# Delta rule: a longer pipeline for the keys' chain, and one merge for both halves of a head

## The chip, the cores and the metric

The kernel runs on one core of one Trainium2 chip. The time is device microseconds of one execution; it is given as the median of several runs. TensorE (PE) multiplies, VectorE (DVE), ScalarE (ACT) and GpSimd (POOL) do the elementwise work, and SyncE (SP) issues all DMAs from one queue, in order. Each engine works through its own queue in order and waits there for the others.

## The reference

Four residual layers on x of 1024 x 1024 in float32: a gated convolution, forgetting attention, gated DeltaNet, sliding-window attention. The change is in the third layer alone. For each of 8 heads of width 128, in 16 chunks of 64 tokens:

```python
qkv = silu(causal_conv(h @ w_in[:, :3072], w_conv))        # q, k, v; q and k are then normalized
L = where(strict, (k_beta @ k.T) * decay, 0)               # per chunk, 64 x 64
T = triangular_solve(eye + L, eye)                         # the inverse
u, w = T @ v_beta, T @ (k_beta * exp(g_cum))
# scan over the chunks
v_new = u_c - w_c @ state
o = qd @ state + qk_c @ v_new
state = state * exp(g_last) + kd.T @ v_new
...
return (rms_norm(o) * w_onorm * silu(z)) @ w_out
```

## The kernel before

**Units.** A projection of 128 features for half of the tokens (512) is eight *units*. A unit is three matmuls of 128 x 512 (L159 to L161): float32 numbers are split into a high and a low part, and high x high, high x low and low x high are added in PSUM. The order of TensorE is written by hand: generators yield after each unit, and `layer_gdn` takes from them in turn. In the steps of phase one the orders of ScalarE and GpSimd are the program's too. VectorE's and SP's orders are a scheduler's, fixed before the run.

**Phase one** makes the keys. Step n (1 to 15; 16 and 17 drain) treats one half of one head, `keys(hd, h)`. Its stages: eight units, then on ACT a copy (L1297) and a product (L1305) and on VectorE three convolution products (L1307); ACT's tanh and VectorE's last product (L1314); then four transposes on TensorE (L1322), which wait for L1314. ACT sums squares (L1330), VectorE (L1361), GpSimd (L1362, a power) and VectorE again (L1364) make the factors; a small transpose (L1379) turns the factors into a row that goes through DRAM and comes back broadcast; GpSimd multiplies it by the decay (L1387); TensorE forms k k^T (L1392), VectorE multiplies (L1394), and the result L goes to DRAM. The stages of several halves are in flight, each a step or two behind the next. Between them stand units of the gate z (`zfill`, weights in the tiles `cv` and `QK`), whose next weights are loaded and split on the way (ACT casts the high part, GpSimd subtracts, L1676).

**The solve.** The 32 x 32 diagonal blocks of eight halves (four heads) lie over 128 partitions. VectorE inverts them row by row: a product of two SBUF tensors (L1428), a reduction (L1431), 80 of them for a block of heads in 71 yields, then a copy (L1434). `advance(b, n)` takes n yields. The first block of heads is solved in steps 10 to 15; the result goes to DRAM (L1433, L1435) and is read back by `loads` (L1459, L1461). Clearing the tile for the second block (L1417) waits until the first result has been written out.

**Phase two** runs the scan, head by head, one half at a time. `prepare` is the fill between the scan's steps: units of q and v, and `merge`, which makes 128 x 128 inverses out of the 32 x 32 blocks in four groups of small matmuls (L1477; L1482 and L1485; L1493; L1498) with VectorE or ACT between them. The scan's hops (L1591, L1596, L1604, then L1623 and L1624) hang together through VectorE; a quota of fill, `FILL // HOPS` = 100 with 64 for a unit, stands between two hops. Each half has its own merge.

Of the kernel before, what the change touches and what calls it, by code (L numbers as in the profile page):

```python
# [16 lines left out]
ALU = mybir.AluOpType  # L17
# [1169 lines left out]
class Gdn:  # L1187
# [249 lines left out]

    def advance(self, b, n):

        if b not in self.sol:  # L1440
            self.sol[b] = self.solve(b, self.U)
        for _ in range(n):
            if next(self.sol[b], 0) == 0:
                break

    def loads(self, hd, h):

        k, p, nc = self.k, self.p, self.nc
        LT = p.tile([P, HT], F32, name="LT", bufs=3)
        nc.sync.dma_start(out=LT.rearrange("p (c i) -> p c i", i=P), in_=self.chunks(self.LT_d[hd][h]))  # L1450
        TT = p.tile([P, 4, P], F32, name="TT", bufs=NB)
        nc.gpsimd.memset(TT, 0.0)
        T1 = p.tile([P, 4, 64], F32, name="T1", bufs=1)
        nc.gpsimd.memset(T1, 0.0)
        base = (hd % 4) * 32 + h * 16
        for q in range(4):
            qs = slice(32 * q, 32 * q + 32)
            src = [self.T_d[hd // 4][t][base:base + 16, :].rearrange("(c q) (r n) -> q r c n", q=4, n=32)[q] for t in range(2)]
            nc.sync.dma_start(out=TT[qs, :, qs], in_=src[1])  # L1459
            if q < 3:  # L1460
                nc.sync.dma_start(out=T1[qs, :, 32:64] if q == 1 else T1[qs, :, 0:32], in_=src[0])  # L1461
        kT = p.tile([P, HT], F32, name="kT", bufs=NB)
        nc.sync.dma_start(out=kT, in_=self.kT_d[hd][h])
        return LT, TT, T1, kT

    def merge(self, LT, TT, T1):

        k, p, nc = self.k, self.p, self.nc
        LT = LT.rearrange("p (c i) -> p c i", i=P)
        ps = k.psum("pj")  # L1470
        v32 = lambda a, rows: ps[rows, a:a + 128].rearrange("p (c n) -> p c n", n=32)
        fst = [slice(64 * q, 64 * q + 32) for q in range(2)]
        snd = [slice(64 * q + 32, 64 * q + 64) for q in range(2)]
        Q = p.tile([P, 4, 32], F32, name="Q", bufs=1)
        for q in range(2):
            for c in range(4):
                nc.tensor.matmul(v32(0, snd[q])[:, c, :], LT[fst[q], c, snd[q]], T1[fst[q], c, 0:32], start=True, stop=True)  # L1477
        for q in range(2):
            nc.vector.tensor_scalar(Q[snd[q]], v32(0, snd[q]), -1.0, None, op0=ALU.mult)
        yield 16  # L1480
        for c in range(4):
            nc.tensor.matmul(v32(128, snd[0])[:, c, :], TT[snd[0], c, snd[0]], Q[snd[0], c, :], start=True, stop=True)  # L1482
        for q in range(2):
            for c in range(4):
                nc.tensor.matmul(v32(128, fst[q])[:, c, :], Q[snd[q], c, :], TT[snd[q], c, snd[q]], start=True, stop=True)  # L1485
        nc.scalar.copy(T1[snd[0], :, 0:32], v32(128, snd[0]))
        for q in range(2):
            nc.scalar.copy(TT[fst[q], :, snd[q]], v32(128, fst[q]))
        yield 40
        lo, up = slice(0, 64), slice(64, 128)  # L1490
        v64 = lambda rows: ps[rows, 256:512].rearrange("p (c n) -> p c n", n=64)
        for c in range(4):
            nc.tensor.matmul(v64(up)[:, c, :], LT[lo, c, up], T1[lo, c, :], start=True, stop=True)  # L1493
        Q6 = p.tile([P, 4, 64], F32, name="Q6", bufs=1)
        nc.vector.tensor_scalar(Q6[up], v64(up), -1.0, None, op0=ALU.mult)
        yield 18
        for c in range(4):
            nc.tensor.matmul(v64(lo)[:, c, :], Q6[up, c, :], TT[up, c, up], start=True, stop=True)  # L1498
        nc.scalar.copy(TT[lo, :, up], v64(lo))
        yield 44  # L1500


    def wload(self, j, hd):
# [3 lines left out]
    def prepare(self, hd, h):  # L1507

        k, p, nc = self.k, self.p, self.nc
        hs = slice(h * HT, (h + 1) * HT)  # L1510
        LT, TT, T1, kT = self.ahead.pop(0)
        E = p.tile([P, HT], F32, name="LT", bufs=3)
        nc.sync.dma_start(out=E, in_=self.E_d[hd][h])
        eg = p.tile([P, HT], F32, name="LT", bufs=3)
        nc.sync.dma_start(out=eg, in_=self.eg_d[hd:hd + 1, hs].broadcast_to([P, HT]))
        mg = self.merge(LT, TT, T1)

        def mixed(steps, vals, every):
# [12 lines left out]

        first = hd == 0
# [6 lines left out]
        yield from mg  # L1539
        if h:  # L1540
            self.wload(2, hd + 1)
        nxt = hd * 2 + h + 1
        if nxt < 16:
            self.ahead.append(self.loads(nxt // 2, nxt % 2))
# [12 lines left out]
        self.vals.append((v, hd, h))  # L1557
        self.prep[hd, h] = [kT, TT, q, sq, QK]
# [89 lines left out]

FILL = 1300
HOPS = 13  # L1650
ZF = 5
LAG = 5

MORE = (25, 0, -25)
# [2 lines left out]
def layer_gdn(k, out):  # L1657
    with k.tc.tile_pool(name="gd", bufs=1) as p:
# [52 lines left out]
        with k.tc.manual_schedule(engines={E_.PE}):  # L1711
# [13 lines left out]
            stage(0, 5)  # L1725
            take(gts)
            stage(0, 4)
            take(zfill, ZF + 5)
            take(gts)
            take(zfill, 3)  # L1730
            take(gts)
# [3 lines left out]

            def step(n):
                hd, h = n // 2, n % 2
                dec = decs.pop(0)
# [9 lines left out]
                if n > 1:  # L1748
                    take(dec)
                if 10 <= n < 16:  # L1750
                    g.advance(0, 6)
                take(cur, 5)
                stage(n - 1, 2)
                take(cur, 4 if n < 16 else 3)
                if n == 1:
                    take(late, 2)
                    take(dec)
                stage(n - 1)
                stage(n - 2)
                if n < 14 and not h:  # L1760
                    kraw.append([k.raw_wk(g.w_in[j * 512:(j + 1) * 512, 1024 + (hd + 1) * P:1024 + (hd + 2) * P], P) for j in range(2)])
                if 10 <= n < 16:
                    g.advance(0, 3)
# [4 lines left out]
                decs.append(g.decay((n + 1) // 2, (n + 1) % 2) if n < 15 else none)  # L1768
                take(decs[0])
                stage(n - 2)  # L1770
                stage(n - 1)
                if 10 <= n < 16:
                    g.advance(0, 3)
# [5 lines left out]
            decs = [g.decay(0, 1)]  # L1779
            take(decs[0])  # L1780
            kraw = [[k.raw_wk(g.w_in[j * 512:(j + 1) * 512, 1024 + P:1024 + 2 * P], P) for j in range(2)]]
            with k.tc.manual_schedule(engines={E_.Activation, E_.Pool}):
                for n in range(1, 16):
                    step(n)
            g.ahead.append(g.loads(0, 0))
            for j in range(2):
                g.kd_load(j)
            step(16)
            step(17)
            stage(15)  # L1790
# [95 lines left out]
```

## Time and profile before

| | us |
|---|---|
| median of 3 runs | 2152.6 (2151.2 to 2155.11) |
| profiled execution, its own time | 2149.09 |
| its span in the trace | 2147.4 |
| TensorE busy | 2078.8 (97% of the span) |
| VectorE busy | 1323.6 (62%) |
| ScalarE busy | 992.1 (46%) |
| GpSimd busy | 836.8 (39%) |
| the chain that ended last | TensorE 74%, VectorE 13%, ACT 4%, DMA 4%, issue 3% |

The phase one of the third layer lies at about 1077 to 1268 us of the span, phase two at about 1268 to 1600. Matmuls are pipelined: the end of a row is modelled, so the time that one takes is read from the start of one row to the start of the next.

### The profile page before, as it was taken

Reading aid. Unit: us, or ns where it says so; the run is one execution under the profiler, and the core shown is the slowest. Engines: PE = TensorE matmul, PEld = TensorE weight load, DVE = VectorE, ACT = ScalarE, POOL = GpSimd, SP = SyncE. Lnnn points to the kernel's source line nnn. Section 1 sums busy time; section 2 is a strip of 40 time slices with the busy share of each in tenths; the row PEclk is TensorE's granted clock in tenths of the full one; section 3 lists DMA queues with packets and bytes.
Section 4 is the critical chain, followed back from the end, with each engine's and each line's share of the span. In section 5 each row is a group of like instructions: output and inputs, shape, how many; then the busy total and the mean of one; then the engine's idle time right before and its main releaser. Section 6 shows DMA issues by size and latency. Waiting matters only on the chain.

```text
span 2147.4 us, 33391 instructions
## 1 busy us (share of the span) xinstructions
PE 2078.8 (97%) x11717; PEld 1748.3 (81%) x11717; DVE 1323.6 (62%) x2748; ACT 992.1 (46%) x2483; POOL 836.8 (39%) x721
## 2 busy tenths in 40 slices
PE   7999999999999999999999789999999999999998
PEld 5887888788898989888688677878888888878888
DVE  7657655544535355475455967775565568888874
ACT  6333334433433233454366443434443446666764
POOL 2244544731221221236356552322324545445630
PEclk9999999999999999999999999999999999999999
DMA  7122213741222321236256553342325521121134
GB/s 237 50 69 84 64 59 119 224 95 41 47 38 44 40 51 31 58 95 187 75 159 195 157 171 96 87 122 78 102 80 164 168 66 49 46 54 50 45 89 148
DMA packets 288366, 205.70 MB, mean 96 GB/s; under 512 B 41381, under 2 KB 245574, under 8 KB 288198
## 3 DMA queue, kind: packets, MB, share of 16 engines
q1 hardware_dynamic: 288198, 203.56, 33.9%
q8 instruction: 93, 1.52, 0.3%
q14 instruction: 75, 0.61, 0.1%
HBM read 154.87 MB, written 43.38 MB: 92 GB/s over the span
## 4 chain that ended last, share of the span: by engine, by line
PE 74%; DVE 13%; ACT 4%; DMA 4%; issue 3%; POOL 1%; SPq 0%; ACTq 0%; POOLq 0%; DVEq 0%
PE ps_pj L159 15%; PE ps_pj L160 15%; PE ps_pj L161 15%; PE ps_sc L248 2%; PE ps_sc L250 2%; PE ps_sc L249 2%; PE ps_pj L248 1%; PE ps_pj L249 1%; PE ps_pj L250 1%; PE ps_tr L835 1%; DVE sp L1428 1%; DVE cu L1307 1%; DVE lg L1153 1%; PE ps_pj L743 1%; PE ps_pj L745 1%
## 5 line engine op out<-in xcount | busy, mean ns | idle before, releaser
L159 PE MATMUL ps_pj<-hhi,whi 128*128 128x512 f32 (+1 forms) x1712 | 698.8, 409 | 3.5 <-ACT hhi L411 1.4
L160 PE MATMUL ps_pj<-hlo,whi 128*128 128x512 f32 (+1 forms) x1712 | 669.2, 391 | 7.2 <-DVE hlo L416 3.9
L161 PE MATMUL ps_pj<-hhi,wlo 128*128 128x512 f32 (+1 forms) x1712 | 669.0, 391 | 0.0
L143 POOL TENSOR_TENSOR wlo<-wraw,whi 128x512 fp32r<-128x512 f32 x296 | 404.4, 1373 | 615.9 <-ACT whi L142 584.9
L161 PEld LDWEIGHTS ps_pj<-hhi,wlo 128*128 128x128 f32 x1712 | 321.8, 188 | 68.9
L160 PEld LDWEIGHTS ps_pj<-hlo,whi 128*128 128x128 f32 x1712 | 323.3, 189 | 61.6 <-DVE hlo L416 5.1
L159 PEld LDWEIGHTS ps_pj<-hhi,whi 128*128 128x128 f32 x1712 | 323.1, 189 | 59.7 <-issue 2.5
L142 ACT CAST whi<-wraw 128x512 fp32r<-128x512 f32 x304 | 185.9, 617 | 312.1 <-PE ps_pj L160 172.7
L1307 DVE SCALAR_TENSOR_TENSOR cu<-cb,taps,cu 128x512 f32<-128x512 f32 x144 | 135.7, 942 | 12.3 <-ACT cu L1305 10.5
L1159 POOL TENSOR_TENSOR lg<-lg,st 128x512 f32<-128x512 f32 (+1 forms) x64 | 63.7, 996 | 122.7 <-DVE st L1158 117.3
L888 ACT ACTIVATE lg<-lg,mx 128x512 f32<-128x512 f32 (+2 forms) x96 | 58.7, 613 | 64.0 <-DVE mx L883 63.6
L1156 ACT ACTIVATE lg<-lg,st 128x257 f32<-128x257 f32 (+1 forms) x128 | 63.1, 494 | 49.2 <-DVE st L1153 49.0
L840 ACT CAST phi<-ps_tr 128x512 fp32r<-128x512 f32 (+1 forms) x80 | 40.6, 544 | 94.3 <-PE ps_tr L835 94.2
L461 DVE TENSOR_TENSOR y<-ps_pj,xr 128x512 f32<-128x512 f32 x56 | 38.5, 687 | 64.0 <-PE ps_pj L161 57.5
L841 DVE TENSOR_TENSOR plo<-ps_tr,phi 128x512 fp32r<-128x512 f32 (+1 forms) x80 | 49.5, 633 | 42.5 <-ACT phi L840 42.5
L469 DVE TENSOR_TENSOR acc<-acc,hf 128x512 f32<-128x512 f32 x49 | 48.5, 990 | 41.2 <-ACT hf L468 41.2
L143 POOL TENSOR_TENSOR wlo<-wr,whi 128x512 fp32r<-128x512 f32 x36 | 48.0, 1333 | 59.0 <-ACT whi L142 54.7
L1428 DVE TENSOR_TENSOR sp<-sT,sU 128x504 f32<-128x504 f32 (+18 forms) x80 | 57.0, 713 | 6.3 <-DMA sU<-gLT 5.1
L1153 DVE CUSTOM_DVE_ANT_0 lg<-ps_sc,band,sk 128x256 f32<-128x256 f32 (+1 forms) x128 | 55.0, 464 | 5.0 <-PE ps_sc L1148 3.4
L291 DVE SCALAR_TENSOR_TENSOR y<-y,ps_pj 128x512 f32<-128x512 f32 x48 | 32.7, 681 | 38.6 <-ACT y L290 38.6
L743 PE MATMUL ps_pj<-whi,hhi 128*128 128x256 f32 x192 | 54.8, 285 | 0.0
L744 PE MATMUL ps_pj<-wlo,hhi 128*128 128x256 f32 x192 | 54.6, 285 | 0.0
(448 smaller groups left out, 4613.5 us busy)
## 6 DMA issues: line engine op xcount, KB each, us to landing
xd<-y SPq DMA_DIRECT2D x64, 256.0 KB, 3.4
wraw<-in_fox_w_in_dram SPq DMA_DIRECT2D x60, 256.0 KB, 4.2
xr<-xd SPq DMA_DIRECT2D x56, 256.0 KB, 2.8
wraw<-in_gdn_w_in_dram SPq DMA_DIRECT2D x52, 256.0 KB, 3.7
wraw<-in_conv_w_in_dram SPq DMA_DIRECT2D x40, 256.0 KB, 3.0
wraw<-in_swa_w_in_dram SPq DMA_DIRECT2D x40, 256.0 KB, 2.9
wraw<-in_conv_w_out_dram SPq DMA_DIRECT2D x32, 256.0 KB, 4.9
wraw<-in_fox_w_out_dram SPq DMA_DIRECT2D x32, 256.0 KB, 2.8
```

The costliest lines, as they stand in the source:

```text
L142: nc.scalar.copy(hi[:, :, :cols], raw[:, :, :cols])
L143: (eng or nc.gpsimd).tensor_tensor(lo[:, :, :cols], raw[:, :, :cols], hi[:, :, :cols].bitcast(F32), op=ALU.subtract)
L159: nc.tensor.matmul(o, hi, xhi, start=(c == 0), stop=False)
L160: nc.tensor.matmul(o, hi, xlo, start=False, stop=False)
L161: nc.tensor.matmul(o, lo, xhi, start=False, stop=(c == NC_ - 1))
L248: nc.tensor.matmul(ps, whi[:, c, :], xhi, start=start and c == 0, stop=False, skip_group_check=True)
L249: nc.tensor.matmul(ps, whi[:, c, :], xlo, start=False, stop=False, skip_group_check=True)
L250: nc.tensor.matmul(ps, wlo[:, c, :], xhi, start=False, stop=stop and c == 3, skip_group_check=True)
L743: nc.tensor.matmul(ps, xhi, whi, start=(c == 0), stop=False)
L1153: nc.vector.tensor_tensor_reduce(lg[:, u, :n], ps[:, u, :n], band[:, 2 * P - n:], 1.0, sk[:, hd:hd + 1], ALU.add, ALU.min, st[:, 0, u:u + 1])
L1307: eng.scalar_tensor_tensor(u, cb[:, j:j + HT], tap(j), u, op0=ALU.mult, op1=ALU.add)
L1428: nc.vector.tensor_tensor(v, T[:, n0:i, n0:n1].rearrange("p j n -> p n j"), U[:, n0:i, i].unsqueeze(1).broadcast_to([P, n, m]), op=ALU.mult)
```

## The change

In phase one the keys' chain gets longer. The transposes of the half before now come after all eight units of the step's own half, and k k^T is formed in the third step behind the half's own, where it was in the second. The gate units between are no longer five in each step: `ZF` = 3 up to step 9, and `ZL` = 8 from step 10 on, in two groups of four. The solve's yields are spread by the table `ROWS` over three places of a step, 65 in steps 10 to 15, the rest in step 16. The decay's rows are loaded in the step itself, not one ahead.

In phase two both halves of a head are merged in one pass through the four groups, while the first half's v is projected. So the second half's blocks are loaded in the middle of the first half's q, the tile T1 has two buffers, and the tiles Q and Q6 go (T1 takes their place). E and eg are loaded at other places.

```diff
     def advance(self, b, n):
-        if b not in self.sol:
+        if n and b not in self.sol:
...
-        T1 = p.tile([P, 4, 64], F32, name="T1", bufs=1)
+        T1 = p.tile([P, 4, 64], F32, name="T1", bufs=2)
...
-    def merge(self, LT, TT, T1):
+    def merge(self, sets):
...
+        sets = [(LT.rearrange("p (c i) -> p c i", i=P), TT, T1, k.psum("pj")) for LT, TT, T1 in sets]
+        for LT, TT, T1, ps in sets:
+            for q in range(2):
+                for c in range(4):
+                    nc.tensor.matmul(v32(ps, 0, snd[q])[:, c, :], LT[fst[q], c, snd[q]], T1[fst[q], c, 0:32], ...)
+            for q in range(2):
+                nc.vector.tensor_scalar(T1[snd[q], :, 0:32], v32(ps, 0, snd[q]), -1.0, None, op0=ALU.mult)
+        yield 16 * len(sets)
...
+        yield 40 * len(sets)
...
+        yield 18 * len(sets)
...
+        yield 44 * len(sets)
...
     def prepare(self, hd, h):
-        mg = self.merge(LT, TT, T1)
...
+                if n == load:
+                    self.ahead.append(self.loads(hd, 1))
...
-        q = yield from mixed(self.conv_steps(self.w[0], hd, h, "qT", 2), LAG, 0 if first else 2)
+        q = yield from mixed(self.conv_steps(self.w[0], hd, h, "qT", 2), LAG, 0, 0 if h else LAG + 1)
         if h:
             self.wload(0, hd + 1)
-        if not first:
-            yield from mg
-        v = yield from mixed(self.conv_steps(self.w[2], 16 + hd, h, "cv", 2), 0, 2)
+        else:
+            mg = self.merge([t[:3] for t in self.ahead])
+        v = yield from mixed(self.conv_steps(self.w[2], 16 + hd, h, "cv", 2), 0, 0 if h else 2)
         yield from mg
...
-ZF = 5
+ZF, ZL = 3, 8
+ROWS = {10: (0, 6, 6), 11: (4, 4, 4), 12: (4, 4, 4), 13: (4, 3, 3), 14: (4, 3, 3), 15: (3, 3, 3), 16: (99,)}
...
             def step(n):
-                stage(n - 2)
-                stage(n - 3)
...
-                take(cur, 5)
-                stage(n - 1, 2)
-                take(cur, 4 if n < 16 else 3)
...
+                take(cur, 2)
+                stage(n - 3)
+                take(dec)
+                take(cur, 3)
+                stage(n - 3)
+                stage(n - 2)
+                solve()
+                if n in ROWS:
+                    take(zfill, ZL // 2)
+                take(cur, 4 if n < 16 else 3)
+                stage(n - 3)
+                stage(n - 2)
...
+                stage(n - 1, 2)
...
-                take(zfill if n < 17 else fill, ZF)
+                take(zfill if n < 17 else fill, ZF if n < 10 else ZL - ZL // 2 if n < 17 else 5)
```

Three places show what moves. The first is TensorE in the middle of the solve's steps, where k k^T (L1392) and the small transpose (L1379) stand. Weights `whi` and `wlo` are a keys' unit, `cv` and `QK` a gate unit. Before:

```order
L161 MATMUL ps_pj<-hhi_0_75,QK 128x512
L1392 MATMUL ps_sc<-kT 128x128 x4
L1379 MATMUL ps_ov<-ident,kq 4x128
L159 MATMUL ps_pj<-hhi_1_2920,whi 128x512
L160 MATMUL ps_pj<-hlo_1_2921,whi 128x512
```

and changed:

```order
L161 MATMUL ps_pj<-hhi_1_84,wlo 128x512
L1392 MATMUL ps_sc<-kT 128x128 x4
L1379 MATMUL ps_ov<-ident,kq 4x128
L159 MATMUL ps_pj<-hhi_1_2920,cv 128x512
L160 MATMUL ps_pj<-hlo_1_2921,cv 128x512
L161 MATMUL ps_pj<-hhi_1_2920,QK 128x512
```

Before, k k^T stands between the gate units and the next step's keys. Now it stands after the first five units of the keys, and four gate units follow.

The second is VectorE at the end of the first solve, from the copy of its result (`sU<-sT`) on; `kT` is the keys' last product, `rk` their norm's. Before:

```order
L1434 COPY sU<-sT 128x1024
L1364 TENSOR_TENSOR kq<-cols,rk 128x16
L1307 SCALAR_TENSOR_TENSOR cu<-cb,taps,cu 128x512 x3
L1417 MEMSET sT 128x1024
L1394 TENSOR_TENSOR LT<-ps_sc,qT 128x512
L1418 MEMSET sT 128x32
L291 SCALAR_TENSOR_TENSOR y_1_2822<-y_1_2822,ps_pj 128x512
L1314 SCALAR_TENSOR_TENSOR kT<-kT,cu 128x512
L1361 TENSOR_SCALAR rk<-rk 128x4
L291 SCALAR_TENSOR_TENSOR y_0_2916<-y_0_2916,ps_pj 128x512
```

and changed, from the last product of keys 14:

```order
L1314 SCALAR_TENSOR_TENSOR kT<-kT,cu 128x512
L1434 COPY sU<-sT 128x1024
L1417 MEMSET sT 128x1024
L291 SCALAR_TENSOR_TENSOR y_0_2821<-y_0_2821,ps_pj 128x512
L1418 MEMSET sT 128x32
L1394 TENSOR_TENSOR LT<-ps_sc,qT 128x512
L1299 MEMSET cb 128x3
L1307 SCALAR_TENSOR_TENSOR cu<-cb,taps,cu 128x512 x2
L1361 TENSOR_SCALAR rk<-rk 128x4
L1307 SCALAR_TENSOR_TENSOR cu<-cb,taps,cu 128x512
```

The last product of keys 14 (L1314), which was done ten rows ahead of the copy, now stands directly ahead of it, and the clearing of sT (L1417) moved from behind the three products L1307 to directly behind the copy; the norm's L1361 stands behind it and two of the products.

The third is TensorE in phase two, at a merge; names beginning with T are the block tiles T1, `TT` the inverse in the making. Before:

```order
L1477 MATMUL ps_pj<-T_13142,LT 32x32 x8
L159 MATMUL ps_pj<-hhi_1_2924,whi 128x512
L160 MATMUL ps_pj<-hlo_1_2925,whi 128x512
L161 MATMUL ps_pj<-hhi_1_2924,wlo 128x512
L159 MATMUL ps_pj<-hhi_1_2926,whi 128x512
L160 MATMUL ps_pj<-hlo_1_2927,whi 128x512
L161 MATMUL ps_pj<-hhi_1_2926,wlo 128x512
L1596 MATMUL ps_sc<-r,TT 128x128
L1482 MATMUL ps_pj<-Q,TT 32x32 x4
L1485 MATMUL ps_pj<-TT,Q 32x32 x8
L159 MATMUL ps_pj<-hhi_1_84,whi 128x512
```

and changed:

```order
L1479 MATMUL ps_pj<-T_12389,LT 32x32 x8
L1479 MATMUL ps_pj<-T_12496,LT 32x32 x8
L159 MATMUL ps_pj<-hhi_0_79,whi 128x512
L160 MATMUL ps_pj<-hlo_0_95,whi 128x512
L161 MATMUL ps_pj<-hhi_0_79,wlo 128x512
L1609 MATMUL ps_sc<-sn,kT 128x128
L159 MATMUL ps_pj<-hhi_0_81,whi 128x512
L160 MATMUL ps_pj<-hlo_0_97,whi 128x512
L161 MATMUL ps_pj<-hhi_0_81,wlo 128x512
L1485 MATMUL ps_pj<-T_12389,TT 32x32 x4
L1488 MATMUL ps_pj<-TT,T_12389 32x32 x8
L1485 MATMUL ps_pj<-T_12496,TT 32x32 x4
```

Where one half's group of eight stood between units, the groups of both halves now follow each other.

## Rows read from the trace of the kernel before

**Rows 1.** Stretches; columns: window, then us and (count) by engine, PEclk, DMA, GB/s.
```profile
1080.68:1173.89 93.21, 93.21 (x461) 77.14 (x460) 52.47 (x73) 62.45 (x204) 61.72 (x68) 1.00 0.63 190
1173.89:1260.96 87.07, 68.78 (x313) 55.16 (x312) 77.08 (x132) 43.32 (x137) 54.71 (x50) 0.94 0.57 161
1300.00:1590.00 290.00, 283.93 (x2177) 234.42 (x2177) 196.42 (x431) 120.86 (x392) 84.91 (x107) 0.99 0.34 95
```

**Rows 2.** Waits of PE, 1080 to 1261 us: total, times, longest.
```profile
PE ps_tr L1322 <- DVE kT L1314: 15.0, 5, 5.2
PE ps_pj L161 <- POOL QK L1676: 2.7, 1, 2.7
```

**Rows 3.** Timeline of PE: start, us, engine, line, operation, tiles, shapes, count.
```profile
1163.42 0.60 PE L1322 MATMUL ps_tr<-ident,kT 128*128 128x128 f32 x4
...
1173.89 0.60 PE L1322 MATMUL ps_tr<-ident,kT 128*128 128x128 f32 x4
...
1181.73 0.40 PE L159 MATMUL ps_pj<-hhi,whi 128*128 128x512 f32 x1
...
1182.42 0.40 PE L159 MATMUL ps_pj<-hhi,whi 128*128 128x512 f32 x1
...
1260.96 0.60 PE L1322 MATMUL ps_tr<-ident,kT 128*128 128x128 f32 x4
```

**Rows 4.** Timeline of DVE, first and last row of the first solve.
```profile
1178.65 0.16 DVE L1428 TENSOR_TENSOR sp<-sT,sU 128x1 f32<-128x1 f32 x1 [5.13 <-DMA sU<-gLT]
...
1249.77 1.14 DVE L1434 COPY sU<-sT 128x1024 f32<-128x1024 f32 x1
```

**Rows 5.** Groups of DVE, 1178.6 to 1251 us: count, busy us, mean ns, idle before.
```profile
L1307 DVE SCALAR_TENSOR_TENSOR cu<-cb,taps,cu 128x512 f32<-128x512 f32 x15 | 14.9, 995 | 0.0
...
L1394 DVE TENSOR_TENSOR LT<-ps_sc,qT 128x512 f32<-128x512 f32 x5 | 3.4, 677 | 0.0
```

**Rows 6.** Timeline of ACT, the product behind a keys' projection.
```profile
1135.28 0.70 ACT L1305 ACTIVATE cu<-ps_pj,taps 128x512 f32<-128x512 f32 x1
```

**Rows 7.** Timeline of POOL and DVE: two products of 49 elements.
```profile
1181.99 1.75 POOL L1387 TENSOR_TENSOR qT<-qT,TT 128x512 f32<-128x512 f32 x1
...
1182.50 1.34 DVE L1428 TENSOR_TENSOR sp<-sT,sU 128x49 f32<-128x49 f32 x1
...
1229.62 0.23 DVE L1428 TENSOR_TENSOR sp<-sT,sU 128x49 f32<-128x49 f32 x1
```

**Rows 8.** Timeline of POOL, SP and DVE around the solve's end; the power earlier.
```profile
1134.63 1.01 POOL L1362 TENSOR_TENSOR rk<-rk,mhalf 128x4 f32<-128x4 f32 x1 [1.09 <-DVE rk L1361]
...
1249.76 0.34 SPq L1433 DMA_DIRECT2D gT<-sT  x1
...
1253.31 0.40 SPq L1461 DMA_DIRECT2D T<-gT  x1
...
1254.50 1.73 POOL L1676 TENSOR_TENSOR QK<-os,cv 128x512 fp32r<-128x512 f32 x1
...
1255.26 0.91 DVE L1417 MEMSET sT<- 128x1024 f32 x1 [0.16 <-DMA gkd<-vb]
```

**Rows 9.** Timeline of PE around one group of a merge in phase two.
```profile
1446.12 0.40 PE L161 MATMUL ps_pj<-hhi,wlo 128*128 128x512 f32 x1
1446.44 0.67 PE L1493 MATMUL ps_pj<-T,LT 64*64 64x64 f32 x8
1447.05 0.50 PE L159 MATMUL ps_pj<-hhi,whi 128*128 128x512 f32 x1
1447.38 0.39 PE L160 MATMUL ps_pj<-hlo,whi 128*128 128x512 f32 x1
```

**Rows 10.** Waits of PE, 1300 to 1600 us: total, times, longest.
```profile
PE ps_sc L1591 <- DVE sn L1609: 5.7, 11, 1.5
```

**Rows 11.** SP's timeline; DMA table: count, KB each, us to landing.
```profile
1258.16 1.92 SPq L1459 DMA_DIRECT2D TT<-gT  x4
...
TT<-gT SPq DMA_DIRECT2D x12, 16.0 KB, 2.2
```

More of the change, by code (lines that the diff above doesn't have):

```diff
@@ L1464, in loads @@
         return LT, TT, T1, kT
-    def merge(self, LT, TT, T1):
[L1468 to L1471, printed above, removed]
+    def merge(self, sets):
+        k, nc = self.k, self.nc
         fst = [slice(64 * q, 64 * q + 32) for q in range(2)]
         snd = [slice(64 * q + 32, 64 * q + 64) for q in range(2)]
-        Q = p.tile([P, 4, 32], F32, name="Q", bufs=1)
-        for q in range(2):
-            for c in range(4):
[L1477 to L1483, printed above, removed]
-            for c in range(4):
[L1485 to L1500, printed above, removed]
@@ new lines, in merge @@
+        yield 16 * len(sets)
+        for LT, TT, T1, ps in sets:
+            for c in range(4):
+                nc.tensor.matmul(v32(ps, 128, snd[0])[:, c, :], TT[snd[0], c, snd[0]], T1[snd[0], c, 0:32], start=True, stop=True)
+            for q in range(2):
+                for c in range(4):
+                    nc.tensor.matmul(v32(ps, 128, fst[q])[:, c, :], T1[snd[q], c, 0:32], TT[snd[q], c, snd[q]], start=True, stop=True)
+            nc.scalar.copy(T1[snd[0], :, 0:32], v32(ps, 128, snd[0]))
+            for q in range(2):
+                nc.scalar.copy(TT[fst[q], :, snd[q]], v32(ps, 128, fst[q]))
@@ new lines, in merge @@
+        yield 40 * len(sets)
+        for LT, TT, T1, ps in sets:
+            for c in range(4):
+                nc.tensor.matmul(v64(ps, up)[:, c, :], LT[lo, c, up], T1[lo, c, :], start=True, stop=True)
+            nc.vector.tensor_scalar(T1[up], v64(ps, up), -1.0, None, op0=ALU.mult)
+        yield 18 * len(sets)
+        for LT, TT, T1, ps in sets:
+            for c in range(4):
+                nc.tensor.matmul(v64(ps, lo)[:, c, :], T1[up, c, :], TT[up, c, up], start=True, stop=True)
+            nc.scalar.copy(TT[lo, :, up], v64(ps, lo))
@@ L1510, in prepare, with decay, growth, mixed @@
         hs = slice(h * HT, (h + 1) * HT)
[L1511 to L1515, printed above, removed]
-        mg = self.merge(LT, TT, T1)
-        def mixed(steps, vals, every):
+        def decay():
+            E = p.tile([P, HT], F32, name="LT", bufs=3)
+            nc.sync.dma_start(out=E, in_=self.E_d[hd][h])
+            return E
+        def growth():
+            eg = p.tile([P, HT], F32, name="LT", bufs=3)
+            nc.sync.dma_start(out=eg, in_=self.eg_d[hd:hd + 1, hs].broadcast_to([P, HT]))
+            return eg
+        mg = ()
+        def mixed(steps, vals, every, load=0):
             n = 0
@@ L1727, in layer_gdn @@
             stage(0, 4)
-            take(zfill, ZF + 5)
+            take(zfill, 10)
             take(gts)
@@ L1737, in step @@
                 hd, h = n // 2, n % 2
-                dec = decs.pop(0)
+                dec = g.decay(hd, h) if n < 16 else none
                 if n < 16:
@@ L1742, in step @@
                     cur = zfill if n == 16 else fill
-                stage(n - 2)
-                stage(n - 3)
+                rows = list(ROWS.get(n, ()))
+                solve = lambda: rows and g.advance(0, rows.pop(0))
                 if n < 15 and h:
@@ L1767, in step @@
                     take(cur)
-                decs.append(g.decay((n + 1) // 2, (n + 1) % 2) if n < 15 else none)
-                take(decs[0])
-                stage(n - 2)
                 stage(n - 1)
-                if 10 <= n < 16:
-                    g.advance(0, 3)
+                solve()
                 if n == 14:
@@ L1777, in step @@
                     g.wload(2, 0)
-            decs = [g.decay(0, 1)]
-            take(decs[0])
             kraw = [[k.raw_wk(g.w_in[j * 512:(j + 1) * 512, 1024 + P:1024 + 2 * P], P) for j in range(2)]]
@@ L1784, in layer_gdn @@
                     step(n)
+            step(16)
             g.ahead.append(g.loads(0, 0))
@@ L1787, in layer_gdn @@
                 g.kd_load(j)
-            step(16)
             step(17)
-            stage(15)
+            stage(15, 3)
             take(zfill, 30)
```

31 lines of the change are left out of this document (18 added, 13 removed).

## The prediction

> **What bounds the kernel now.** I read three views in this order. The table by stretch comes first: it shows where TensorE stands idle or runs at the lower clock, and there alone can a reordering win. In the first nine steps of the keys' chain (1080.68 to 1173.89) TensorE is busy 93.21 of 93.21 us. In the six steps after them (1173.89 to 1260.96) it is busy 68.78 of 87.07 us, at a granted clock of 0.94 against 1.00, while VectorE is busy 77.08 of the 87.07. In phase two (1300 to 1590) TensorE is busy 283.93 of 290 us [rows 1]. The second view is the list of waits: in phase one TensorE waits for the keys' last product on VectorE (L1314) and once for a split of a gate's weights on GpSimd (L1676) [rows 2]. So the six steps that carry the solve are VectorE's, the rest is TensorE's.
>
> The size of that loss comes from the third view, the timeline: the starts of the transposes L1322, of which there is one group to a step [rows 3]. An undisturbed step takes 1173.89 - 1163.42 = 10.47 us. Six of them would be 62.8 us; they take 1260.96 - 1173.89 = 87.07, so 24.3 us are lost. This holds the waits, the time at 1.2 GHz (0.94 is a mean of the two levels; the engine had stood idle in this stretch and not in the one before), and the starts after a wait. It is more than the 18.3 us of idle time because a row of TensorE ends later than the next one may start.
>
> **The change, phase one.** No instruction of the keys goes; they move. One gate unit is three matmuls, 1182.42 - 1181.73 = 0.69 us [rows 3]. Before, each step had 8 units of the keys and 5 of the gates. Now steps 1 to 9 have 3 gate units and steps 10 to 16 have 8. So the first nine steps fall to 10.47 - 2 x 0.69 = 9.1 us, and the steps with the solve grow to 10.47 + 3 x 0.69 = 12.54. TensorE's own work is the same in all. What changes is the cover beside VectorE.
>
> Does VectorE now fit? Before, the solve ran from its first row at 1178.65 to the end of the copy of its result, 1249.77 + 1.14 = 1250.91: 72.3 us [rows 4]. VectorE was busy nearly throughout, so that is its work. In the changed order the same stretch holds 13 products L1307 where it held 15 (0.995 each), 4 products L1394 where it held 5 (0.677), one gate product L291 more, which reads PSUM too and is taken at the same 0.677, and otherwise the same [rows 5]: 72.3 - 2.0 - 0.7 + 0.7 = 70.3 us, 69.2 without the copy. It starts about 3.4 us after the keys of step 10 leave TensorE: an ACT copy and an ACT product, 0.70 each [rows 6], then two products of 0.995. L1314 of keys 14 now stands right before the copy, so it ends 3.4 + 69.2 = 72.6 us after that moment. TensorE needs it after five steps, 5 x 12.54 = 62.7. So 9.9 us of waits are left. The longer pipeline gives more room between a projection and its transposes, but that room is spent once; the rate of VectorE decides.
>
> The rate rests on one slow-down. A product of the solve with 49 elements took 1.34 us at 1182.50 and 0.23 at 1229.62; beside the first, GpSimd ran L1387 for 1.75 us [rows 7]. L1394, which reads PSUM, keeps its 0.677. The Trainium skill ("GPSIMD Engine Reference", section "Key points") says that GpSimd shares its SBUF interfaces with VectorE and contends with VectorE operations that have two SBUF inputs. By that rule the change has a price: 8 gate units a step instead of 5 bring about three more weight splits into the solve's stretch, at 1.73 us [rows 8] up to 5 us more on VectorE, and the sum below would be 13 us instead of 18. The trace agrees with the rule in these two rows; how much of a split falls beside such products no row tells, so it is left out of the sum and stands in the range.
>
> Second, the end of the solve. The two pieces of VectorE's order show that the clearing of the solve's tile (L1417) moves from behind the three products of the next keys to right behind the copy, ahead of L1361. It must wait until the solve's result has left SBUF: issued at 1249.76, its first reader issued at 1253.31 [rows 8], so at most 3.55 us. From the end of L1314: that issue is about 0.8 us earlier, so the clearing starts at 2.7 and takes 0.9; L291 and L1394 1.3, two L1307 2.0, L1361 0.2: 7.1. Behind it GpSimd does the power (1.01) and then the second split of the last gate's weights (1.73): 9.8. TensorE wants that split after its transposes (0.60 by their row), two times four units (5.5) and two matmuls (0.5): 6.6. That is 3.2 us of waiting; before it was 2.7, and is in the 24.3.
>
> Third, the clock. At 1.2 GHz for a part of 0.94's stretch (2 x 0.06 x 87 = 10 us), of which TensorE was busy only in part, the bounds of its cost before are 0 and 5 us. With waits of half the size I take 1.5 us for what is left, with 0 and 3 as bounds. All other moved items I cost at nothing: the keys' loads, stores and decay rows have one step more than before, and GpSimd is busy 54.71 of 87.07 us and 61.72 of 93.21. If that cover failed, a weight split late by its own 1.73 us would show in every second step.
>
> Phase one: 24.3 - 9.9 - 3.2 - 1.5 = 9.7 us won. Bounds: VectorE without contention (24 won), and with 5 us more there and 3 for the clock (3 won).
>
> **The change, phase two.** 16 merges of four groups of small matmuls become 8 of four groups twice as long, with the same matmuls: 64 entries become 32. One entry's price: from L161 at 1446.12 to L160 at 1447.38 are 1.26 us; the two wide matmuls in it (L161, L159) take a third of a unit each, 0.46, the eight small passes (0.67 - 0.22) / 7 = 0.064 each if the last has 0.22, 0.51. The rest, 0.29 us, is entering and leaving [rows 9]. About half the groups stand against other narrow matmuls, where the late start behind L159 (0.33 to L160 instead of 0.23) is paid anyhow. 32 x 0.29 = 9.3 at most, 32 x 0.19 = 6.1 at least; I take 8, nearer the price that the rows show. The VectorE and ScalarE operations are the same in number. The waits of the scan for its state, 5.7 us in all [rows 10], depend on what fill lies in each hop; halves without a merge have shorter hops, those with one longer, so I leave them, with 3 us either way.
>
> **Sum.** 9.7 + 8 = 17.7 us. The profiled execution took 2149.09 us (its span 2147.4 and 1.7 around it), 3.5 under the median of 2152.6: 2131.4 for it, 2135 for the median.
>
> **Rivals.** (a) VectorE keeps up. If the solve's slow-downs mostly vanish, as the pair of rows allows (1.11 us in one operation), because longer steps leave more time between GpSimd's operations, the waits at L1314 and the clock's part go: 24.3 - 3.2 + 8 = 29.1 us, 2123.5. Against it: VectorE had hardly an idle moment to compress. (b) Phase one gives back nearly all: contention with the three splits (5 us) and 3.0 instead of 1.5 for the clock, and phase two at its lower price. 9.7 - 6.5 + 6.1 = 9.3 us, 2143.3. For it speaks that GpSimd is no idler in the solve's steps than ahead of them. (c) Slower: the merge of both halves waits for the inverse blocks of the second half. Its tile comes free only when the scan has used the one of three halves before; then a memset, four issues (1.92 us) and a landing (2.2) follow [rows 11], about 5 us. TensorE's order has seven units (4.8 us) and some 4 us of narrow matmuls between that last use and the second half's part of the merge, 8.8, so nothing waits. If the four issues stand more than 3.8 us behind others in SP's queue, each further microsecond is paid in seven heads: from 17.7 / 7 = 2.5 us more on (6.3 of delay) the kernel is slower, at 8 us of delay by 12, 2164. Against it: in phase two the DMA engines are busy 0.34 of the time [rows 1]. (d) No change that can be measured, if (b) meets 5 us of such waits: 2149.
>
> **How the numbers follow.** The forecast has 0.50, with a range of its own of 2128 to 2142; (a) 0.20, (b) 0.17, (c) 0.06, (d) 0.07. No change means within 0.2%, 4.3 us, about what a measurement of this kernel can tell. The forecast, (a) and most of (b) are faster: 0.84; same 0.09; slower 0.07. The range reaches over (b) and (a): 2120 to 2149.
>
> **What would show it.** Right: gate units by three and by eight, steps of about 9.1 us before the solve and 12.5 to 15 in it; waits at L1322 for L1314 still there in the later solve steps, some 10 us; one wait for the split of the last gate's weights of about 3 us; 32 groups of small matmuls. Wrong: no wait for L1314 at all (then (a)), a new wait of TensorE for the loads of TT or T1 in phase two (then (c)), or steps before the solve that are longer than 9.1 us.

## The result and the profile after

The changed kernel takes 2173.88 us (median of 4 runs, 2167.26 to 2176.02) against 2152.4 before: ratio 1.0093, 95% interval 1.0069 to 1.0117. It is slower by 0.9%, and I had forecast 2135. The profiled execution has a span of 2172.8 us against 2147.4.

Where the time went is read from four starts on TensorE. The last L1274, just ahead of the keys, starts at 1077.1 before and 1078.7 after: 1.6 us lie ahead of the changed code. From there to the scan's first L1591 (L1609 after) it is 219.2 us before (1296.3) and 237.7 after (1316.4): 18.5 are lost in phase one and at the entry of phase two. From there to the scan's last L1623 (L1641) it is 336.0 and 339.5 us, 3.5 more, and from there to the last matmul of all 1.1 more. That is 24.7, all but 0.7 of the difference of the spans.

The table by stretch, of the changed kernel. The first row holds the steps ahead of the solve, the second the one in which the solve begins, the third the other steps with it, the fourth the scan (columns as in [rows 1]).

```profile
1084.24:1168.29 84.05, 74.80 (x361) 61.82 (x360) 37.92 (x61) 52.12 (x178) 47.56 (x56) 0.96 0.55 166
1168.29:1186.03 17.74, 13.54 (x59) 11.04 (x58) 6.10 (x9) 6.58 (x22) 8.62 (x10) 0.90 0.61 189
1186.03:1278.17 92.14, 80.59 (x368) 65.39 (x367) 77.02 (x135) 45.53 (x142) 52.40 (x52) 0.94 0.50 150
1316.40:1655.90 339.50, 321.77 (x2437) 269.11 (x2438) 232.92 (x484) 136.71 (x436) 97.37 (x119) 0.99 0.32 89
```

Before, TensorE had no idle time in the steps ahead of the solve [rows 1]; now it is idle 84.05 - 74.80 = 9.3 us there and 4.2 in the next row. In the scan it is idle 17.7 us. The same row of before, from the scan's first hop to its last:

```profile
1296.30:1632.30 336.00, 329.58 (x2491) 272.67 (x2492) 220.86 (x485) 137.86 (x440) 99.85 (x120) 0.99 0.33 91
```

There it was 6.4. TensorE's busy time fell by 7.8 us and its idle time grew by 11.3. (The records fell from 2491 to 2437 because the merge of the first head's second half, 56 records and 3.0 us busy, lies ahead of the scan now. So about 3 of the 7.8 us are only moved.)

The list of waits of TensorE in the changed kernel from 1080 to 1186, to be read against [rows 2]:

```profile
PE ps_ov L1379 <- DVE kq L1364: 11.2, 3, 4.2
PE ps_ov L1379 <- ACT TT L1347: 2.2, 1, 2.2
```

and from 1186 to 1316, those of more than 0.5 us (the 3.5 us at L1479 lie at the entry of phase two, at 1293):

```profile
PE ps_ov L1379 <- DVE sp L1428: 3.6, 1, 3.6
PE ps_pj L1479 <- issue: 3.5, 1, 3.5
PE ps_ov L1379 <- ACT kT L1313: 2.6, 1, 2.6
PE ps_ov L1379 <- DVE kq L1364: 2.4, 1, 2.4
PE ps_ov L1379 <- DVE sT L1431: 1.3, 1, 1.3
PE ps_pj L159 <- ACT cv L1696: 1.0, 1, 1.0
PE ps_pj L161 <- POOL QK L1697: 0.6, 1, 0.6
```

The wait for the keys' last product (15.0 us in [rows 2]) is gone. In its place TensorE waits at the small transpose L1379, for the factors `kq`: 13.4 us ahead of the solve, where it never waited before, and 9.9 in it.

What holds `kq` ahead of the solve is seen in one timeline over all engines, one step of the changed kernel (columns as in [rows 3]; the bracket is the idle time before the row and what ended it):

```profile
1101.49 1.29 POOL L1387 TENSOR_TENSOR qT<-qT,TT 128x512 f32<-128x512 f32 x1
...
1103.60 0.38 SPq L1340 DMA_DIRECT2D TT<-g_d  x1
...
1108.63 0.63 POOL L1342 TENSOR_SCALAR_AFFINE_SELECT TT<-TT 128x512 f32<-128x512 f32 x1 [5.73 <-DMA TT<-g_d]
1109.24 1.01 POOL L1362 TENSOR_TENSOR rk<-rk,mhalf 128x4 f32<-128x4 f32 x1
...
1110.28 1.24 DVE L1364 TENSOR_TENSOR kq<-cols,rk 128x16 f32<-128x16 f32 x1 [4.41 <-POOL rk L1362]
...
1111.66 0.37 PE L1379 MATMUL ps_ov<-ident,kq 128*4 128x128 f32 x1 [3.27 <-DVE kq L1364]
1113.13 1.28 POOL L1387 TENSOR_TENSOR qT<-qT,TT 128x512 f32<-128x512 f32 x1
```

Read it upwards from L1379. `kq` waits for the power L1362 on GpSimd. The power has its operand, and stands behind the selection L1342, which waits 5.73 us for the decay row of this step. That row is loaded (L1340) into a tile TT, of which there are three, and the tile comes free when the multiply L1387 has read the row of three halves ago. The loads follow those multiplies: the one at 1113.13 ends at 1114.41, and the next load is issued at 1114.43; the next multiply ends at 1127.15, and its load is issued at 1127.17. Before, the same ring was as tight, but the load stood one step ahead of its use:

```profile
1107.20 1.28 POOL L1387 TENSOR_TENSOR qT<-qT,TT 128x512 f32<-128x512 f32 x1 [0.49 <-DMA qT<-gbr]
...
1108.51 0.32 SPq L1340 DMA_DIRECT2D TT<-g_d  x1
...
1112.00 0.64 POOL L1342 TENSOR_SCALAR_AFFINE_SELECT TT<-TT 128x512 f32<-128x512 f32 x1 [1.80 <-DMA TT<-g_d]
1113.73 1.01 POOL L1362 TENSOR_TENSOR rk<-rk,mhalf 128x4 f32<-128x4 f32 x1 [1.10 <-DVE rk L1361]
```

There GpSimd waited for the row too, but the power still waited for its own operand afterwards (1.10), and TensorE came to L1379 at 1118.08 without a wait.

### The profile page after: what moved, and what is told of

The parts are those of the page before. It is cut to its first block, busy times and chain, and to the rows that moved or that the text cites. A ratio compares the mean times of both kernels' runs of the same rounds, so it can differ in the third digit from the quotient of the medians.

```text
span 2172.8 us, 33361 instructions
## 1 busy us (share of the span) xinstructions
PE 2080.0 (96%) x11717; PEld 1752.5 (81%) x11717; DVE 1323.0 (61%) x2748; ACT 989.1 (46%) x2483; POOL 826.7 (38%) x721
## 5 line engine op out<-in xcount | busy, mean ns | idle before, releaser
L159 PE MATMUL ps_pj<-hhi,whi 128*128 128x512 f32 (+1 forms) x1712 | 695.3, 407 | 3.4 <-ACT whi L142 1.3
L161 PE MATMUL ps_pj<-hhi,wlo 128*128 128x512 f32 (+1 forms) x1712 | 669.3, 391 | 0.0
L143 POOL TENSOR_TENSOR wlo<-wraw,whi 128x512 fp32r<-128x512 f32 x296 | 402.7, 1366 | 600.1 <-ACT whi L142 569.0
L161 PEld LDWEIGHTS ps_pj<-hhi,wlo 128*128 128x128 f32 x1712 | 322.3, 188 | 68.8
L159 PEld LDWEIGHTS ps_pj<-hhi,whi 128*128 128x128 f32 x1712 | 323.4, 189 | 59.3 <-issue 3.0
L1307 DVE SCALAR_TENSOR_TENSOR cu<-cb,taps,cu 128x512 f32<-128x512 f32 x144 | 120.6, 837 | 24.5 <-ACT cu L1305 23.3
L143 POOL TENSOR_TENSOR wlo<-wr,whi 128x512 fp32r<-128x512 f32 x36 | 48.0, 1333 | 60.2 <-ACT whi L142 54.8
L291 DVE SCALAR_TENSOR_TENSOR y<-y,ps_pj 128x512 f32<-128x512 f32 x48 | 32.7, 681 | 39.9 <-ACT y L290 39.9
```

Of the source, the lines that this page charges most:

```text
L143: (eng or nc.gpsimd).tensor_tensor(lo[:, :, :cols], raw[:, :, :cols], hi[:, :, :cols].bitcast(F32), op=ALU.subtract)
L159: nc.tensor.matmul(o, hi, xhi, start=(c == 0), stop=False)
L161: nc.tensor.matmul(o, lo, xhi, start=False, stop=(c == NC_ - 1))
L1307: eng.scalar_tensor_tensor(u, cb[:, j:j + HT], tap(j), u, op0=ALU.mult, op1=ALU.add)
```

## The experiments

Two theories on the loss in phase one, **ring** (the three tiles of the decay rows) and **splits** (GpSimd and ScalarE late in the shorter steps), and two on phase two stood at the beginning. Ratios are to the kernel before, measured beside each run. Differences in us are of medians; for runs of different series the ratios can give some 4 us more or less. Single profiles differ too: from the last L1274 to the last L1379 it is 190.9 us in the kernel before and 193.1 in the control run below, whose phase one is the same, so a difference of 2 us between two traces says little.

**A fourth tile.** The two buffers of T1, which phase one doesn't use, become one tile of the size of a decay row, and every fourth half's row goes there.

```diff
-        E = p.tile([P, HT], F32, name="TT", bufs=NB)
+        E = p.tile([P, HT], F32, name="T1") if h and hd % 2 == 0 else p.tile([P, HT], F32, name="TT", bufs=NB)
...
-        T1 = p.tile([P, 4, 64], F32, name="T1", bufs=2)
+        if h == 0:
+            self.T1 = p.tile([P, 2, 4, 64], F32, name="T1")
+        T1 = self.T1[:, h]
```

> The changed kernel with a fourth tile for the decay rows of phase one (every fourth half uses the tile of T1, of which both buffers are one tile here; same memory). Theory ring: the load of a half's decay row waits until the multiply L1387 of three halves earlier has freed its tile, in the same step in which GpSimd wants the row, and the power behind it on GpSimd holds up TensorE's L1379. Then the four waits of 3.3, 2.2, 3.8 and 4.2 us in the steps before the solve go, with a part of the later ones and of the half clock: 2154 to 2160 us, no wait of TensorE at L1379 before the solve. Rival splits: GpSimd and ScalarE are simply late with the splits of the keys' weights since these steps are shorter (9.1 us); then the time stays at 2174 and the waits stay.

Measured: 2157.89 us, ratio 1.0038 (1.0026 to 1.0051), 16.0 less than the change, 12 by the ratios. Phase one's waits of TensorE, 1080 to 1262:

```profile
PE ps_ov L1379 <- DVE sp L1428: 6.8, 2, 5.3
PE ps_ov L1379 <- DVE sT L1431: 4.1, 1, 4.1
PE ps_ov L1379 <- DVE kq L1364: 2.7, 1, 2.7
PE ps_pj L161 <- POOL QK L1699: 0.7, 1, 0.7
```

None of them lies ahead of 1173: the nine steps before the solve run at (1161.0 - 1088.7) / 8 = 9.04 us from L1379 to L1379, without idle time. From the last L1274 to the scan it is 224.1 us instead of 237.7. This shows the ring, and that the splits were not what was late.

**The same link cut at another place.** The tiles stay, and GpSimd does the power first.

```diff
-                take(dec)
                 stage(n - 1, 2)
+                take(dec)
...
-                take(dec)
                 if n < 16:
                     take(cur)
                 stage(n - 1)
+                take(dec)
```

> The changed kernel with GpSimd's L1342 (which waits for the decay row) behind the power L1362 instead of ahead of it, and ScalarE's L1347 at the end of the step; the tiles as they are, so the load is as late as before. Theory ring with the order on GpSimd as the link: TensorE's waits at L1379 for kq go as in the run with a fourth tile, 2154 to 2162, and GpSimd waits just as long at L1342. If the late row itself is what counts (the multiply L1374 or L1387 then comes late), the wait moves to L1394 and nothing is won: 2170 or more.

Measured: 2167.4 us, 1.0069 (1.0048 to 1.0091). Up to 1160 TensorE's waits shrink to 0.5 us, so GpSimd's order is the link: the ninth L1379 starts at 1163.4 instead of 1179.5. Half of this is lost again in the solve's steps: the last L1379 starts at 1278.0 instead of 1285.7. There a gate's split is late by 1.3 us (L161 for L1697) and a gate's cast on ScalarE by 3.3 (L159 for L1696, 1.0 in the change); that the late row is behind this is not shown. The time lies between the two theories, 2162 and 2170.

**Each part alone.** The kernel before with phase one of the change (`ZF`, `ZL`, `ROWS` and the steps, as the diff begins) or with phase two of it (`merge`, `loads` and `prepare`; here the last gate units of phase one stand a little ahead).

```diff
-ZF = 5
+ZF, ZL = 3, 8
+ROWS = {10: (0, 6, 6), 11: (4, 4, 4), 12: (4, 4, 4), 13: (4, 3, 3), 14: (4, 3, 3), 15: (3, 3, 3), 16: (99,)}
...
```

> The kernel before with the change of phase one alone (one merge per half as before). Theory ring: all of the loss is here, about 20 us: 2172. Rival: the two parts hurt each other (the last loads of phase one); then under 2162.

Measured: 2163.4 us, 1.0059 (1.0038 to 1.0081), with 12.4 us of waits at L1379 up to 1186. I had expected 2172: not all of the loss is in this part.

> The kernel before with the change of phase two alone (both halves of a head merged together; the last gate units of phase one stand a little ahead). By the traces phase two took 333.4 us before (first to last L1591) and 336.3 after: theory fill (the shorter groups save what was forecast, but the halves without a merge wait in the scan's hops) gives 2155 us. Rival: phase two lost those us only because phase one ended badly (loads, clock); then the forecast 8 us are won, 2145.

Measured: 2155.92 us, 1.0026 (1.0012 to 1.0040). So both parts lose, and not through each other: 0.59% and 0.26%, 13 and 6 us, beside 0.93% (20 us) of the whole change. The scan's length here is 336.6 us, with phase one undisturbed, where 8 us less than 336.0 were forecast, so the rival that blamed the end of phase one falls. (In the changed kernel the scan is 2.9 us longer still, with the same idle time and a granted clock of 0.99 instead of 1.00.) The waits of TensorE in it, 1296 to 1670:

```profile
PE ps_sc L1622 <- DVE vn L1616: 8.7, 9, 1.6
PE ps_sc L1614 <- DVE r L1611: 6.6, 7, 1.4
```

against the 5.7 us at one place in [rows 10]. What VectorE does in the longest of them:

```profile
1439.51 0.69 DVE L1573 TENSOR_TENSOR QK<-ps_tr,LT 128x512 f32<-128x512 f32 x1 [0.98 <-PE ps_tr L1569]
1440.12 1.61 DVE L1307 SCALAR_TENSOR_TENSOR cu<-cb,taps,cu 128x512 f32<-128x512 f32 x1
1441.65 0.28 DVE L1616 COPY vn<-ps_sc 128x128 f32<-128x128 f32 x1
```

The matmul L1614 had started at 1439.31; its copy `vn` came 2.3 us later, behind the product for QK and one of a projection's three products, which took 1.61 us beside a product of GpSimd (L1574, 1.27 us from 1439.91).

**The copy vn on ScalarE**, with the fourth tile (2157.89) as the base. The rows of the second solve that were tied to this copy on VectorE are not tied any more.

```diff
-            ins = nc.vector.tensor_copy(vn, ps[:, P:2 * P])
-            with k.tc.issue_after(ins.ins):
-                self.advance(1, 1)
+            nc.scalar.copy(vn, ps[:, P:2 * P])
+            self.advance(1, 1)
```

> The kernel with the fourth decay tile (2157.9 us) with the scan's copy vn on ScalarE instead of VectorE. In phase two TensorE waits 8.7 us for that copy, which stands on VectorE behind a product L1307 and the product for QK. Theory order of VectorE: the copy is ready when its matmul is done and only queued behind these; on ScalarE the 8.7 us go, 2149 to 2153 us. Rival short hops: the two units in the hop don't cover matmul plus copy wherever the copy is; then TensorE waits as long for ScalarE, 2157.

Measured: 2148.3 us, 0.9983 (0.9972 to 0.9994), 9.6 less than the base, 12 by the ratios. The scan's waits from 1296 to 1670 are now

```profile
PE ps_sc L1616 <- DVE r L1613: 5.5, 8, 1.2
PE ps_sc L1611 <- DVE sn L1628: 2.4, 6, 0.4
PE ps_sc L1623 <- ACT vn L1618: 1.8, 4, 0.7
```

and the scan takes 329.2 us: the hops were long enough, the copy was queued. The same edit in the kernel before, as a control:

> The kernel before with the copy vn on ScalarE alone. In it TensorE waits for sn (6 us) and not for vn. Theory: the loss at vn is made by the change, which puts the ends of projections in front of it; then nothing is won here, 2149 to 2154 beside the before of the same runs. Rival: the copy on ScalarE is better anyway, by the 9.6 us that it gave in the changed kernel: 2142.

Measured: 2150.8 us, 1.0007 (0.9995 to 1.0019): nothing there, and its scan takes 336.6 us, so the loss at `vn` belongs to the change. In phase two of the change alone:

> Phase two of the change alone (2155.9 us) with vn on ScalarE, phase one as before. If the late vn is what ate the gain of the common merge, it wins 7 to 10 us against its own 2155.9, and the forecast's 8 us of phase two stand against the kernel before (2150.2): 2143 to 2148. If the gain was never there: 2150 or more.

Measured: 2147.24 us, 0.9978 (0.9968 to 0.9988), 8.7 less than without. Against the kernel before these are 0.22%, 4.7 us of the 8 that were forecast for phase two.

**The solve behind the keys.** With the fourth tile, one wait of 5.3 us is left in the step in which the solve begins. VectorE there:

```profile
1165.60 0.69 DVE L1394 TENSOR_TENSOR LT<-ps_sc,qT 128x512 f32<-128x512 f32 x1 [2.27 <-POOL qT L1387]
1175.36 0.16 DVE L1428 TENSOR_TENSOR sp<-sT,sU 128x1 f32<-128x1 f32 x1 [9.07 <-DMA sU<-gLT]
1175.43 0.75 DVE L1307 SCALAR_TENSOR_TENSOR cu<-cb,taps,cu 128x512 f32<-128x512 f32 x1
```

The solve's first row waits 9.07 us for the last of its blocks, which the longer pipeline makes a step later (5.13 before, [rows 4], where the next L1379 did not wait), and the keys' products stand behind it.

```diff
-ROWS = {10: (0, 6, 6),
+ROWS = {10: (0, 0, 0),
...
                 stage(n - 1)
                 solve()
+                if n == 10:
+                    with k.tc.issue_after(g.final.ins):
+                        g.advance(0, 12)
```

> The kernel with the fourth decay tile with the first row of the solve behind the last product of keys 10 (L1314) on VectorE. In it VectorE stands 9.07 us at the first row, for the load of the last of the eight blocks, which the longer pipeline makes a step later; the products L1307, L1361 and so TensorE's L1379 (5.3 us) wait behind it. Theory early start: that wait goes, 2152 to 2154. Rival rate: the solve starts and ends later and the us come back at its end, 2157.

Measured: 2151.47 us, 1.0008 (0.9995 to 1.0021), 6.4 less. From the last L1274 to the scan it is 218.3 us (224.1 in the base). Left in phase one are

```profile
PE ps_ov L1379 <- DVE kq L1364: 6.6, 3, 2.9
PE ps_ov L1379 <- ACT kT L1313: 3.1, 1, 3.1
PE ps_pj L161 <- POOL QK L1699: 2.3, 1, 2.3
```

**L1379 later.** Also with the fourth tile: the transpose behind the four gate units that follow it.

```diff
                 stage(n - 3)
-                stage(n - 2)
                 solve()
                 if n in ROWS:
                     take(zfill, ZL // 2)
+                stage(n - 2)
```

> The kernel with the fourth decay tile with the small transpose L1379 behind the four gate units that follow k k^T instead of ahead of them (2.8 us later, steps 10 to 16). It waits 13.6 us there for VectorE (5.3, 2.7, 1.5, 4.2). Theory placed too early: 2.8 + 2.7 + 1.5 + 2.8 = 9.8 us of it go, 2148. Theory rate: VectorE is full during the solve, so what TensorE doesn't wait here it waits later in the solve or after it; at most the wait ahead of the full stretch goes, 2153 to 2157.

Measured: 2160.81 us, 1.0039 (1.0018 to 1.0059), by the ratio level with the base (1.0038). The waits at L1379 shrink to 8.5 us and others come (5.3 for the splits L1699, 1.2 for L291). So what TensorE doesn't wait at L1379 it waits elsewhere, as the second theory had it, though here mostly for GpSimd; that theory's time was still 4 us too low.

**The quota by half.** With the fourth tile.

```diff
-                    quota = FILL // HOPS + (extra or 0)
+                    quota = (110 if i % 2 else 92) + (extra or 0)
```

> The kernel with the fourth decay tile with a quota of fill of 92 to a hop in first halves and 110 in second halves instead of 100 in all. A first half now needs 1432 of fill (two merges) and a second 1196 (none), so with equal quotas the ends of the projections, and VectorE's work at them, fall on another hop in each half. Theory phase: with quotas that follow the fill the hops meet the same work in each half as before the change, and the 18 us of idle time of TensorE in phase two (6.4 before) fall to 8 to 12: 2150 to 2154. Rival order of VectorE alone: the waits only move to other hops, 2155 to 2160.

Measured: 2152.17 us, 1.0009 (0.9997 to 1.0021), 5.7 less. The waits for `vn` fall from 8.7 to 3.3, those for `r` rise from 6.7 to 8.0; the scan takes 332.9 us, of which TensorE is idle 13.5 (8 to 12 expected). So where the ends of the projections fall among the hops counts, and with `vn` on VectorE equal quotas put them ill. Not all of the waits go, so this is part of the cause, not a rival to VectorE's order.

**All together.**

> The changed kernel with all four mends: fourth decay tile, solve behind the last product of keys 10, vn on ScalarE, quota of 92 and 110. If they add up: 2157.9 less 9.6 (vn), 6.4 (solve) and 5.7 (quota) is 2136; the quota and vn share waits in phase two (8.7 of 18 us), so I expect 2137 to 2141. Rival: in phase two both remove the same waits, then the quota adds nothing, 2142 or more.

Measured: 2148.2 us, 0.9987 (0.9976 to 0.9998). They don't add up: the scan takes 334.4 us, with 7.4 us of waits for `r`. Without the quota:

> As the kernel with all four mends, but with the quota of 100 in all hops as in the change. In that kernel phase two took 334.4 us against 329.2 with vn on ScalarE alone: theory interference (the quota was set for hops in which vn was late; with vn on ScalarE it moves a projection's end onto r): without it 2157.9 - 9.6 - 6.4 = 2142, faster than both kernels. Rival: the mend of the solve and that of vn don't add for another reason: 2148 as with four.

Measured: 2142.7 us, 0.9964 (0.9951 to 0.9977), the expected time, with a scan of 329.2 us. It is faster than both kernels: by 0.36%, 8 us, than the kernel before and, ratio against ratio, by 28 us than the change (31 by the medians).

## Why the prediction was wrong

**The step that failed** is "All other moved items I cost at nothing: the keys' loads, stores and decay rows have one step more than before". For the decay rows the opposite is so. The change loads them in the step itself, and the longer pipeline holds each tile up to the multiply of the third step. With three tiles the load can't start before that multiply. I had counted steps and not tiles. What showed in every second step was not the late split that I had named (1.73 us) but the wait for `kq`, 2.2 to 4.2 us. It cost 13.6 us up to the scan (237.7 to 224.1 with a fourth tile), 12 to 16 in the time. The forecast that the steps ahead of the solve fall to 9.1 us was right once that was gone (9.04).

**The second step that failed** is that the waits of the scan stay as they are "with 3 us either way". They went from 6 to 16 us (8.7 for `vn` and 6.9 for `r`), and the gain of the merge went into them. The gain itself was there: with `vn` on ScalarE in both, the scan takes 336.6 us in the kernel before and 328.6 with phase two of the change, 8.0 less. Part of this is not won in the sum, for both merges of the first head lie ahead of the scan now, without hops to hide in: with the same 29 units behind the last L1379 it is 30.6 us from there to the first hop in the run with phase two alone (1269.9 to 1300.5) and 28.4 before (1267.9 to 1296.3), 2.2 more. So the term of 8 us was too large by two to three.

**Phase one, the other terms.** The rate of VectorE came out as worked: from the solve's first row (1189.11) to the copy (1258.39) it took 69.3 us, and 69.2 were forecast. That is partly luck, for its terms did not. Two groups of VectorE in the solve before, beside [rows 5]:

```profile
L1314 DVE SCALAR_TENSOR_TENSOR kT<-kT,cu 128x512 f32<-128x512 f32 x5 | 4.5, 895 | 0.0
L1364 DVE TENSOR_TENSOR kq<-cols,rk 128x16 f32<-128x16 f32 x5 | 0.9, 172 | 0.4 <-POOL rk L1362 0.3
```

and three in the changed one:

```profile
L1307 DVE SCALAR_TENSOR_TENSOR cu<-cb,taps,cu 128x512 f32<-128x512 f32 x13 | 9.8, 754 | 0.0
L1314 DVE SCALAR_TENSOR_TENSOR kT<-kT,cu 128x512 f32<-128x512 f32 x5 | 6.3, 1250 | 0.0
L1364 DVE TENSOR_TENSOR kq<-cols,rk 128x16 f32<-128x16 f32 x5 | 3.0, 602 | 0.4 <-POOL rk L1362 0.4
```

The products L1307 took 0.754 us each where 0.995 was forecast, 3.1 us less, and L1314 and `kq` 3.9 us more. Nor did the three more splits that stood in the range come: four splits of gate weights lie in this stretch where two lay before, but four of the keys' weights (L143) where six lay, and GpSimd is busy 36.3 us in it against 43.1. So this case doesn't test the 5 us that I had put on them.

The waits that this rate leaves were forecast at 9.9 us; they are 9.9 in the change and 9.7 with the solve behind the keys (6.6 and 3.1). That it agrees to a tenth is luck too, for they are at L1379 and not at L1322 for L1314: I had looked for the late engine's last product, and with a step of room behind it the wait stood at another product of the same engine. The granted clock of the solve's steps stayed at 0.94, where I had halved its cost.

The clearing of the solve's tile came later than forecast:

```profile
1256.93 1.54 DVE L1314 SCALAR_TENSOR_TENSOR kT<-kT,cu 128x512 f32<-128x512 f32 x1
...
1257.04 0.32 SPq L1433 DMA_DIRECT2D gT<-sT  x1
...
1262.20 0.91 DVE L1417 MEMSET sT<- 128x1024 f32 x1 [2.73 <-DMA gT<-sT]
```

It starts 3.7 us after the end of L1314 (2.7 forecast) and 5.2 after the issue of the result's store, where I had at most 3.55. The wait for the last gate's weights is nevertheless 1.6 us (1.0 for ScalarE's cast, 0.6 for the split) instead of 3.2. I had not seen that the start of the solve waits longer for its last block: 5.8 us up to the scan (224.1 to 218.3).

**The sum.** Phase one, with these two mends, is worth 2147.24 - 2142.7 = 4.5 us (3.0 by the ratios; phase two is the same in both runs), where 9.7 were forecast. Where the rest is shows in two stretches, from the last L1274 to the last L1379 and from there to the first hop. With phase one as before (columns as in [rows 1]):

```profile
1077.43:1270.90 193.47, 174.54 (x827) 141.71 (x826) 129.05 (x210) 109.44 (x355) 123.13 (x124) 0.96 0.58 171
1270.90:1302.20 31.30, 28.31 (x230) 22.85 (x228) 16.94 (x46) 11.87 (x30) 8.55 (x12) 1.00 0.51 146
```

and in the kernel with three mends:

```profile
1077.74:1267.60 189.86, 175.81 (x850) 144.69 (x849) 120.69 (x213) 107.67 (x353) 118.44 (x123) 0.98 0.59 175
1267.60:1297.10 29.50, 25.04 (x207) 19.78 (x204) 15.52 (x39) 11.99 (x33) 9.06 (x14) 0.94 0.52 149
```

With the change, 21 units stand behind the last L1379 instead of 29; eight units, 5.5 us, lie ahead of it. So the first stretch is 3.6 us shorter with 5.5 us more work in it: 9.1 won, near the forecast. The second is 1.8 us shorter with 5.5 us less work: 3.7 lost. Of these 1.5 are idle time (4.5 us against 3.0) and the rest longer busy time, at a granted clock of 0.94 instead of 1.00. TensorE waits there 2.1 us at L1322 for `cv` (1.2 with phase one as before, 0.3 in the kernel before, and 3.1 in the run with phase one alone). So it seems that these units had covered the entry of phase two, one more moved item that I had costed at nothing; no run moves them alone, and the shares are of single traces.

In the changed kernel the entry loses in another place:

```profile
1293.38 0.84 PE L1479 MATMUL ps_pj<-T,LT 32*32 32x32 f32 x16 [3.47 <-issue]
```

The trace names nothing that ended this wait of the second half's merge. In the run with the power first the same wait, 3.7 us, is put down to the load of LT. That would be the mechanism of rival (c), once and ahead of the scan. Of the rivals none was the one: (c) has the right side, but no wait in the scan is put down to a load.

## What to carry to other kernels

When a pipeline is lengthened, count for each tile the steps from its first write to its last read and compare with the number of its buffers: a buffer that comes free in the step in which its next content is wanted turns a covered load into a wait, and on an engine with a fixed order everything behind it waits too. Work that is taken out of one place of a schedule uncovers what it stood beside and shifts all that follows it: hops that were tuned to one pattern must be looked at again, above all on the engine whose order a scheduler sets. A late engine's wait need not stay at the product where it was: more room behind one product moves it to another.

## What the runs showed of the hardware

The product `kq` has 16 elements in a row. In the changed kernel it took 1.24 us at 1110.28 (above) and 0.17 in another step:

```profile
1190.90 0.17 DVE L1364 TENSOR_TENSOR kq<-cols,rk 128x16 f32<-128x16 f32 x1 [0.44 <-POOL rk L1362]
```

Beside the first, GpSimd ran a split of 128 x 512:

```profile
1110.21 1.28 POOL L1697 TENSOR_TENSOR QK<-os,cv 128x512 fp32r<-128x512 f32 x1
```

It ended at 1111.49, and the product at 1111.52: this operation of VectorE with two SBUF inputs lasted until GpSimd's was over. The Trainium skill ("GPSIMD Engine Reference", section "Key points") names such contention, and the trace agrees: from 1080 to 1260 six products `kq` of the changed kernel ran beside a split and took 1.23 to 1.26 us, the eight others 0.15 to 0.18. So some 1.1 us (1.24 less 0.17) of the wait of 3.27 shown above may be this slow-down: in the changed order the split stands directly behind the power. The 49 elements of [rows 7] took 1.34 us with 1.24 of GpSimd's operation left to run, these 16 took 1.24 with 1.21 left: I had not expected that the price goes by what is left of GpSimd's operation and hardly by VectorE's own length.
